# Window attention in a hybrid decoder layer: the softmax of both key heads of a unit as one chain over eight heads

## The chip, the cores and the metric

The kernel runs on one core of one Trainium2 chip. The core has a matrix engine (PE, whose weight loads are listed apart as PEld), a vector engine (DVE), a scalar engine (ACT), a general engine (POOL) and queues for transfers (DMA), most of them issued from SP. The metric is the device time of one execution in microseconds (us). One execution was also taken with the hardware profiler; every row below is from that one.

## The reference, cut to what matters

One inference step of one layer: a prompt of 2048 rows and a sample group of 8 x 8 rows. One projection of the normalized input gives q, k, v, a gate z and the inputs of a state-space branch. The change touches the window attention of the prompt: 16 query heads of 64 elements share 4 key heads (4 query heads to each), every query sees the 128 keys up to its own, and a learned sink for each head joins the softmax.

```python
def sink_attention(q, k, v, mask, sinks):
    s = jnp.einsum('bnqkgd,bnskd->bnkgqs', q, k).astype(jnp.float32) * (HEAD_DIM ** -0.5)
    s = jnp.where(mask[None, :, None, None], s, -jnp.inf)
    sk = sinks.astype(jnp.float32).reshape(N_KV_HEADS, KV_GROUP)[:, :, None, None]
    m = jnp.maximum(s.max(-1, keepdims=True), sk)
    p = jnp.exp(s - m)
    p = p / (p.sum(-1, keepdims=True) + jnp.exp(sk - m))
    return jnp.einsum('bnkgqs,bnskd->bnqkgd', p.astype(v.dtype), v)
...
o_a = window_attention_prompt(q, k, v, p['sinks'])   # prompt: blocks of 128 queries
p_a = (o_a * jax.nn.silu(z_a)) @ p['w_attn_proj'].astype(o_a.dtype)
```

## The kernel before, in words

The program has three stages. T1 (`phase_t1`) projects q, k, v and the gate z and does the window attention; S does the state-space branch; T2 does the output projections. In the profiled execution T1 lasts to 741 us, S to about 1950 us, T2 to the end.

T1 goes over four blocks of 512 rows, in each over two pairs of key heads, and in each over four units `tt` of 128 queries: 32 units. A unit is 128 queries against two key heads (`kvl` 0 and 1), each with four query heads. For each key head `attn_unit` does the following.

- Scores: eight matmuls of 256 columns (L541) into two PSUM tiles `sc` (the pool `sc1` has two). They hold the older and the newer 128 keys side by side; each query uses one of the two at each place, so ACT copies the newer half to the SBUF tile `s` (L547) and DVE writes the older half over it where it is seen (L548). `s` is 128 queries x 4 heads x 128 keys.
- Softmax: one DVE reduce for the maximum (L553), then the helper `softmax` (L378): the negative maximum `ng` (L380), the sink's part `es` (L382, L383), an exp for each head on ACT that also sums (L386), the denominator `den` on DVE (L387 to L389), and the scaling of each head, two heads on ACT (L391) and two on POOL (L393).
- Four transposes on PE (L558) into a PSUM tile `tr`, and one DVE product with the masks `halves` that writes both halves of `PT` (L560).

When both key heads are there, four matmuls of 512 columns (L570) form the unit's output `po`, DVE multiplies it with the gate (L581), and SP stores it.

Other places that the text speaks of: `za_tile` (gate columns of a pair; in block 2 it also does the columns of the sample group, which pass through the SBUF tile `zt`, one buffer, L447 to L451, and are stored to `zss_d`), `sample_cols` (likewise through `zt`, L425, stored to `qks_d`), `v_tile` (values, and 32 columns for the state-space branch through the tile `dtt`, one buffer of its own, L491), `q_tile` (transposes L515), the projections' matmuls (L186, L199, L210), and the split of raw weights into two parts, a cast on ACT (L150) and a subtraction on DVE (L151). At the start of S, L811 transposes `dA`, whose result is stored to `ac_d` and loaded again as `AB` and `EB`; L902 transposes `xT`.

The order in which instructions stand on each engine is not the order of the code: a scheduler lays the whole program out ahead of time from its own estimates of durations and from the pools' buffers, and each engine then runs its list strictly in that order. The units' softmax work is so laid among the matmuls of projections of the same and the next block.

Of the kernel before, what the change touches and what calls it, by code (L numbers as in the profile page):

```python
# [9 lines left out]
F32 = mybir.dt.float32  # L10
F32R = mybir.dt.float32r
AF = mybir.ActivationFunctionType
ALU = mybir.AluOpType
AX = mybir.AxisListType
# [3 lines left out]
P = 128  # L18
# [4 lines left out]
NT = TB // P  # L23
NH, NKV, HD, HG = 16, 4, 64, 4
# [54 lines left out]
def build(tc, nc, a, o, seq, phases=("T1", "S", "T2"), dbg=None):  # L79
# [296 lines left out]
        )  # L376

    def softmax(wk, s, mx, width, nsk, sk, n):  # L378
        ng = wk.tile([P, 4], F32, name="ng", tag="ng")
        V.scalar_tensor_tensor(out=ng[:, :n], in0=mx[:, :n], scalar=-1.0, in1=nsk, op0=ALU.mult, op1=ALU.min)  # L380
        es_ = wk.tile([P, 4], F32, name="es", tag="es")
        V.tensor_tensor(es_[:, :n], sk, ng[:, :n], ALU.add)  # L382
        A.activation(es_[:, :n], es_[:, :n], AF.Exp)  # L383
        den = wk.tile([P, 4], F32, name="den", tag="den")
        for i in range(n):
            A.activation(s[:, i, :width], s[:, i, :width], AF.Exp, bias=ng[:, i : i + 1], accum_out=den[:, i : i + 1])  # L386
        V.tensor_tensor(den[:, :n], den[:, :n], es_[:, :n], ALU.add)  # L387
        V.tensor_scalar(den[:, :n], den[:, :n], 2.0, None, ALU.mult)
        V.reciprocal(den[:, :n], den[:, :n])  # L389
        for i in range(min(n, 2)):  # L390
            A.activation(s[:, i, :width], s[:, i, :width], AF.Copy, scale=den[:, i : i + 1])  # L391
        for i in range(2, n):
            G.tensor_scalar(s[:, i, :width], s[:, i, :width], den[:, i : i + 1], None, ALU.mult)  # L393

    def phase_t1():
        with ExitStack() as es:
# [9 lines left out]
            qtp = pool("qtp", 3)  # L406
            kvp = pool("kvp", 1)
            zap = pool("zap", 2)
            sp = pool("sp", 5)
            ptp = pool("ptp", 2)  # L410
            smp = pool("smp", 2)
            mmp = pool("mm1", 3, space=PSUM)
# [66 lines left out]
            def v_tile(b, hT):  # L479
                if b == 0:  # L480
                    SY.dma_start(raw_dt, w_in[:, OFF_DT : OFF_DT + 32].rearrange("(k p) c -> p k c", p=P))
                raw, hl = wload([(0, w_in[:, OFF_V : OFF_V + 256])])
                split(hl[:, 0, :, 256:288], hl[:, 1, :, 256:288], raw_dt)
                if b > 0:
                    G.tensor_copy(vT[:, 0], vT[:, 4])
                dtt = wk.tile([P, NT, 32], F32, name="dtt", tag="dtt", bufs=1)
                for tt in range(NT):
                    ps = mmp.tile([P, 288], F32, name="mm", tag="mm")
                    proj_tm(ps, hl, 288, hT, tt)
                    A.copy(vT[:, tt + 1], ps[:, :256])  # L490
                    V.tensor_copy(dtt[:, tt], ps[:, 256:288])  # L491
                SY.dma_start(dt_d[b], dtt)
                if b == NB - 1:
                    SY.dma_start(o["v_win_p"], vT[:, 4])
                if b == sb:
                    sample_cols(raw, lambda t: [(vn_d[:, P * f : P * f + P], t[64 * f : 64 * f + 64]) for f in range(2)])
                    psd = mmp.tile([P, 32], F32, name="mm", tag="mm")
                    for k in range(KT):
                        for f in range(2):
                            PE.matmul(psd[64 * f : 64 * f + 64], hs[:, k], raw_dt[:, k], start=k == 0, stop=k == KT - 1)  # L500
                    V.tensor_copy(dts, psd)
# [25 lines left out]
            def attn_unit(b, pair, tt, qTs, zs):  # L527
                full = b * NT + tt > 0
                k0, W = (tt * P, 256) if full else ((tt + 1) * P, P)
                ws = (0, 1) if full else (1,)  # L530
                PTs = []
                po = trp.tile([P, HG, P], F32, name="tr", tag="tr")
                for kvl in range(2):
                    kv = 2 * pair + kvl
                    s = sp.tile([P, HG, P], F32, name="s", tag="s")
                    mx = smp.tile([P, HG], F32, name="mx", tag="mx")
                    for hh in range(2):
                        sc = scp.tile([P, 2, 256], F32, name="sc", tag="sc")
                        for h in range(2):
                            for i in range(2):  # L540
                                PE.matmul(  # L541
                                    sc[:, h, :W], qTs[kvl][:, 2 * hh + h], KTT[:, i, kv, k0 : k0 + W],
                                    start=i == 0, stop=i == 1,
                                )
                        if full:
                            sv = s[:, 2 * hh : 2 * hh + 2]
                            A.copy(sv, sc[:, :, P:])  # L547
                            V.copy_predicated(sv, older.unsqueeze(1).to_broadcast([P, 2, P]), sc[:, :, :P])  # L548
                        else:
                            for h in range(2):  # L550
                                masked_max(s, mx, 2 * hh + h, sc[:, h, :P], mask, P)
                    if full:
                        V.tensor_reduce(mx, s, AX.X, ALU.max)  # L553
                    softmax(smp, s, mx, P, nsink[:, 4 * kv : 4 * kv + 4], sink[:, 4 * kv : 4 * kv + 4], HG)
                    PT = ptp.tile([P, 2, HG, P], F32, name="PT", tag="PT")
                    tr = trp.tile([P, HG, P], F32, name="tr", tag="tr")
                    for hg in range(HG):
                        PE.transpose(tr[:, hg], s[:, hg], ident)  # L558
                    if full:
                        got = V.tensor_tensor(  # L560
                            PT, tr.unsqueeze(1).to_broadcast([P, 2, HG, P]),
# [803 lines left out]
```

## Time and profile before

| | us |
|---|---|
| median of 3 runs | 3145.01 (3144.47 to 3152.12) |
| the profiled execution's own time | 3143.59 |
| its span on the core | 3141.8 |
| PE busy in the span | 3059.9 (97%) |
| stage T1, PE busy in its first 742 us | 699.63 |

Times in the rows are from the start of the span. "Idle" of an engine is time in which no instruction of it ran; the releaser after `<-` is what ended it. In the orders and rows, L-numbers are lines of the kernel; in the changed kernel the lines of `attn_unit` stand 1 to 3 lines lower or higher (scores L540, transposes L561, `PT` L563, products L573, gate product L584; in S L814 for L811 and L905 for L902).

### The profile page before, as it was taken

Reading aid. Unit: us, or ns where it says so; the run is one execution under the profiler, and the core shown is the slowest. Engines: PE = TensorE matmul, PEld = TensorE weight load, DVE = VectorE, ACT = ScalarE, POOL = GpSimd, SP = SyncE. Lnnn points to the kernel's source line nnn. Section 1 sums busy time; section 2 is a strip of 40 time slices with the busy share of each in tenths; the row PEclk is TensorE's granted clock in tenths of the full one; section 3 lists DMA queues with packets and bytes.
Section 4 is the critical chain, followed back from the end, with each engine's and each line's share of the span. In section 5 each row is a group of like instructions: output and inputs, shape, how many; then the busy total and the mean of one; then the engine's idle time right before and its main releaser. Section 6 shows DMA issues by size and latency. Waiting matters only on the chain.

```text
span 3141.8 us, 49127 instructions
## 1 busy us (share of the span) xinstructions
PE 3059.9 (97%) x18982; PEld 2635.5 (84%) x18982; DVE 1918.5 (61%) x3142; ACT 1356.5 (43%) x2863; POOL 933.1 (30%) x925
## 2 busy tenths in 40 slices
PE   8999999998999999999999998999999999999999
PEld 7979797976999888778877877878878899999888
DVE  5868767677666666676666665456556644333433
ACT  4656545455555444444445453343333322222321
POOL 2425232432455444555554554100111110000000
PEclk9999999999999999999999998999999999999999
DMA  6635345254777755665666564455655663345443
GB/s 223 189 106 148 112 120 166 68 185 154 243 256 259 282 207 202 233 228 188 222 244 212 201 219 142 149 141 172 208 176 144 177 193 123 103 147 159 138 107 104
DMA packets 409986, 553.72 MB, mean 176 GB/s; under 512 B 34145, under 2 KB 347257, under 8 KB 399497
## 3 DMA queue, kind: packets, MB, share of 16 engines
q1 hardware_dynamic: 409752, 550.59, 54.1%
q8 instruction: 149, 2.44, 0.3%
q14 instruction: 85, 0.69, 0.1%
HBM read 445.31 MB, written 107.30 MB: 176 GB/s over the span
## 4 chain that ended last, share of the span: by engine, by line
PE 78%; DVE 8%; DMA 4%; POOL 4%; issue 3%; ACT 2%; SPq 0%; POOLq 0%; DVEq 0%; ACTq 0%
PE mm L199 49%; PE mm L210 13%; PE mm L186 6%; DVE acc L792 2%; PE tr L570 2%; PE sc L541 2%; DVE whl L151 1%; PE py L910 1%; POOL ws L913 1%; POOL L L889 1%; PE tr L558 1%; PE st L916 1%; PE po L898 1%; DMA v<-v_d 1%; DVE zs L929 1%
## 5 line engine op out<-in xcount | busy, mean ns | idle before, releaser
L199 PE MATMUL mm<-hT,whl 128*128 128x512 f32 (+1 forms) x6720 | 1341.4, 355 | 6.1 <-DVE whl L151 3.0
L199 PEld LDWEIGHTS mm<-hT,whl 128*128 128x128 f32 x6720 | 1117.5, 189 | 175.8 <-issue 7.4
L199 PE MATMUL mm<-ot,whl 128*128 128x512 f32 (+1 forms) x2880 | 567.9, 354 | 3.0 <-DVE whl L151 1.4
L199 PEld LDWEIGHTS mm<-ot,whl 128*128 128x128 f32 x2880 | 474.9, 188 | 74.0 <-DVE whl L151 2.9
L151 DVE TENSOR_TENSOR whl<-raw,whl 128x2048 fp32r<-128x2048 f32 (+1 forms) x172 | 366.7, 2137 | 266.5 <-ACT whl L150 259.4
L150 ACT CAST whl<-raw 128x2048 fp32r<-128x2048 f32 (+1 forms) x172 | 298.4, 1746 | 218.0 <-PE mm L199 101.2
L210 PE MATMUL mm<-whl,hT 128*128 128x256 f32 (+1 forms) x2304 | 303.5, 286 | 2.7 <-DVE dtt L491 2.2
L210 PEld LDWEIGHTS mm<-whl,hT 128*128 128x128 f32 x2304 | 286.8, 189 | 7.9 <-issue 4.1
L792 DVE SCALAR_TENSOR_TENSOR acc<-cr,cwb,acc 128x512 f32<-128x512 f32 x288 | 272.5, 948 | 27.3 <-ACT acc L787 24.9
L889 POOL TENSOR_TENSOR L<-L,cbm 128x1024 f32<-128x1024 f32 x64 | 162.2, 2546 | 146.5 <-DVE cbm L878 139.5
L210 PE MATMUL mm<-whl,ot 128*128 128x256 f32 (+1 forms) x1632 | 204.0, 284 | 0.0
L210 PEld LDWEIGHTS mm<-whl,ot 128*128 128x128 f32 (+1 forms) x1632 | 198.8, 188 | 3.7 <-issue 2.1
L186 PE MATMUL mm<-hT,whl 128*128 128x512 f32 x768 | 192.7, 400 | 2.2 <-ACT hT L295 2.1
L887 ACT ACTIVATE L<-AB,acs 128x128 f32<-128x128 f32 x512 | 157.5, 390 | 63.1 <-PE py L910 29.3
L186 PEld LDWEIGHTS mm<-hT,whl 128*128 128x128 f32 x768 | 141.2, 190 | 33.5 <-ACT hT L295 2.5
L859 DVE SCALAR_TENSOR_TENSOR zs<-th,mm 128x512 f32<-128x512 f32 (+1 forms) x80 | 45.6, 577 | 152.4 <-ACT th L858 151.9
L393 POOL TENSOR_SCALAR s<-s,den 128x128 f32<-128x128 f32 x128 | 79.3, 632 | 198.7 <-DVE den L389 144.1
L858 ACT ACTIVATE th<-mm 128x512 f32<-128x512 f32 (+1 forms) x80 | 40.0, 508 | 202.8 <-PE mm L199 196.7
L150 ACT CAST ot<-v 128x512 fp32r<-128x512 f32 x96 | 58.7, 620 | 159.5 <-DVE v L1231 81.0
L386 ACT ACTIVATE s<-s,ng 128x128 f32<-128x128 f32 x256 | 99.9, 394 | 39.9 <-DVE ng L380 32.6
L1231 DVE SCALAR_TENSOR_TENSOR v<-v,snw,rb 128x512 f32<-128x512 f32 x64 | 49.3, 786 | 97.6 <-DMA v<-v_d 97.4
L913 POOL TENSOR_TENSOR ws<-wx,ws 128x512 fp32r<-128x512 f32 x64 | 106.4, 1663 | 5.1 <-ACT ws L912 4.9
(324 smaller groups left out, 3899.6 us busy)
## 6 DMA issues: line engine op xcount, KB each, us to landing
raw<-in_w_in_dram SPq DMA_DIRECT2D x72, 1024.0 KB
whl<-w_dx SPq DMA_DIRECT2D x24, 2048.0 KB
whl<-w_dz SPq DMA_DIRECT2D x24, 2048.0 KB
hT<-h_d SPq DMA_DIRECT2D x80, 512.0 KB
AB<-ac_d SPq DMA_DIRECT2D x64, 512.0 KB
raw<-in_w_ssd_proj_dram SPq DMA_DIRECT2D x32, 1024.0 KB
whl<-w_dbc SPq DMA_DIRECT2D x12, 2048.0 KB
raw<-in_w_in_dram SPq DMA_DIRECT2D x40, 512.0 KB
```

Source lines behind the costliest of these rows:

```text
L150: A.copy(hi, src)
L151: V.tensor_tensor(lo, src, hi.bitcast(F32), ALU.subtract)
L186: PE.matmul(ps, hl[:, x, k, c0 : c0 + P], ht[:, y, :], start=first and i == 0, stop=last and i == n - 1,)
L199: PE.matmul(ps, hl[:, x, k, c0 : c0 + P], ht[:, y, lo : lo + n], start=i == 0, stop=i == 3 * len(hT) - 1,)
L210: PE.matmul(ps, ht[:, x, tt * P : tt * P + m], hl[:, y, k, :n], start=i == 0, stop=i == 3 * len(hT) - 1,)
L386: A.activation(s[:, i, :width], s[:, i, :width], AF.Exp, bias=ng[:, i : i + 1], accum_out=den[:, i : i + 1])
L393: G.tensor_scalar(s[:, i, :width], s[:, i, :width], den[:, i : i + 1], None, ALU.mult)
L541: PE.matmul(sc[:, h, :W], qTs[kvl][:, 2 * hh + h], KTT[:, i, kv, k0 : k0 + W], start=i == 0, stop=i == 1,)
L792: V.scalar_tensor_tensor(out=acc, in0=raw[:, k : k + TB], scalar=cwb[:, k, ct : ct + 1], in1=acc, op0=ALU.mult, op1=ALU.add)
L887: A.activation(L[:, h], AB[:, h], AF.Relu, scale=-1.0, bias=acs[:, hc.start + h : hc.start + h + 1])
L889: G.tensor_tensor(L, L, cbm[:, c].unsqueeze(1).to_broadcast([P, 8, P]), ALU.mult)
L913: G.tensor_tensor(ws[:, 1], wx, ws[:, 0].bitcast(F32), ALU.subtract)
```

## The change

The unit gets one tile `s` of eight heads for both key heads (the pool `sp` goes from five tiles of four heads to three of eight), and `mx`, `ng`, `es` and `den` are eight wide. All scores of the unit are evacuated first; then there is one reduce, one chain of small operations and one exp of the sinks for the unit, eight exps, and the scaling, the first four heads (key head 0) on ACT and the last four (key head 1) on POOL. Transposes and `PT` of both key heads come behind that. Apart from it, `dtt` takes its place in the one buffer of `zt`.

```diff
     def softmax(wk, s, mx, width, nsk, sk, n):
-        ng = wk.tile([P, 4], F32, name="ng", tag="ng")
+        ng = wk.tile([P, 8], F32, name="ng", tag="ng")
...
-        for i in range(min(n, 2)):
+        for i in range((n + 1) // 2):
             A.activation(s[:, i, :width], s[:, i, :width], AF.Copy, scale=den[:, i : i + 1])
-        for i in range(2, n):
+        for i in range((n + 1) // 2, n):
             G.tensor_scalar(s[:, i, :width], s[:, i, :width], den[:, i : i + 1], None, ALU.mult)
...
-            sp = pool("sp", 5)
+            sp = pool("sp", 3)
...
-                dtt = wk.tile([P, NT, 32], F32, name="dtt", tag="dtt", bufs=1)
+                dtt = wk.tile([P, NT, 32], F32, name="dtt", tag="zt", bufs=1)
...
+                s = sp.tile([P, 2 * HG, P], F32, name="s", tag="s")
+                mx = smp.tile([P, 2 * HG], F32, name="mx", tag="mx")
                 for kvl in range(2):
                     kv = 2 * pair + kvl
-                    s = sp.tile([P, HG, P], F32, name="s", tag="s")
-                    mx = smp.tile([P, HG], F32, name="mx", tag="mx")
                     for hh in range(2):
...
+                        at = HG * kvl + 2 * hh
                         if full:
-                            sv = s[:, 2 * hh : 2 * hh + 2]
+                            sv = s[:, at : at + 2]
...
-                    if full:
-                        V.tensor_reduce(mx, s, AX.X, ALU.max)
-                    softmax(smp, s, mx, P, nsink[:, 4 * kv : 4 * kv + 4], sink[:, 4 * kv : 4 * kv + 4], HG)
+                if full:
+                    V.tensor_reduce(mx, s, AX.X, ALU.max)
+                heads = slice(2 * HG * pair, 2 * HG * pair + 2 * HG)
+                softmax(smp, s, mx, P, nsink[:, heads], sink[:, heads], 2 * HG)
+                PTs = []
+                for kvl in range(2):
                     PT = ptp.tile([P, 2, HG, P], F32, name="PT", tag="PT")
...
-                        PE.transpose(tr[:, hg], s[:, hg], ident)
+                        PE.transpose(tr[:, hg], s[:, HG * kvl + hg], ident)
```

The instructions of PE, POOL and the transfers keep their numbers; DVE has 2952 in place of 3142 and ACT 2549 in place of 2581. The order of the rest of S and of T2 is the same on every engine; that of T1 and of the first 30 us of S is new. At three places it stands as follows.

PE at the end of block 1 (its last units, called 13, 14 and 15 below, before the keys and values of block 2). Before, from the product of unit 13 (the L210 are projections of block 2, the L449 transposes of `zt`):

```order
L570 MATMUL tr<-PT,vT 64x512 x4
L210 MATMUL mm<-whl,hT 128x288 x20
L558 MATMUL tr<-cst,s 128x128
L210 MATMUL mm<-whl,hT 128x288
L558 MATMUL tr<-cst,s 128x128 x2
L210 MATMUL mm<-whl,hT 128x288 x3
L558 MATMUL tr<-cst,s 128x128 x5
L210 MATMUL mm<-whl,hT 128x288 x24
L570 MATMUL tr<-PT,vT 64x512 x4
L449 MATMUL tr<-cst,zt 128x128
L210 MATMUL mm<-whl,hT 128x288 x24
L449 MATMUL tr<-cst,zt 128x128
```

After, from the last scores of the block:

```order
L540 MATMUL sc<-KTT,qT 128x256 x8
L573 MATMUL tr<-PT,vT 64x512 x4
L210 MATMUL mm<-whl,hT 128x288 x24
L561 MATMUL tr<-cst,s 128x128 x8
L573 MATMUL tr<-PT,vT 64x512 x4
L561 MATMUL tr<-cst,s 128x128 x8
L573 MATMUL tr<-PT,vT 64x512 x4
L449 MATMUL tr<-cst,zt 128x128 x2
L472 MATMUL tr<-cst,kd 128x128 x4
L210 MATMUL mm<-whl,hT 128x288 x27
```

Before, 72 matmuls of 288 columns stood between the product of unit 13 and the second L449; after, 24, and the two L449 stand together.

The end of the first pair of block 3 (units 26 and 27, before the query transposes L515 of the second pair). DVE before, and then after:

```order
L560 TENSOR_TENSOR PT<-tr,halves 128x1024
L151 TENSOR_TENSOR whl<-raw,whl 128x2048 x2
L151 TENSOR_TENSOR hT<-hs,hT 128x64 x4
L560 TENSOR_TENSOR PT<-tr,halves 128x1024
L151 TENSOR_TENSOR hT<-hs,hT 128x64 x2
L581 TENSOR_TENSOR zs<-tr,zs 128x4x128
```

```order
L563 TENSOR_TENSOR PT<-tr,halves 128x1024
L151 TENSOR_TENSOR whl<-raw,whl 128x2048 x2
L151 TENSOR_TENSOR hT<-hs,hT 128x64 x2
L548 COPY_PREDICATED s<-cst,sc 128x256
L151 TENSOR_TENSOR hT<-hs,hT 128x64
L548 COPY_PREDICATED s<-cst,sc 128x256
L151 TENSOR_TENSOR hT<-hs,hT 128x64 x3
L584 TENSOR_TENSOR zs<-tr,zs 128x4x128
L553 TENSOR_REDUCE mx<-s 128x8
L380 SCALAR_TENSOR_TENSOR ng<-mx,nsink 128x8
```

PE at the same place, before and then after (the L186 are the last matmuls of a projection):

```order
L541 MATMUL sc<-KTT,qT 128x256 x4
L186 MATMUL mm<-hT,whl 128x512 x17
L570 MATMUL tr<-PT,vT 64x512 x4
L558 MATMUL tr<-cst,s 128x128 x8
L570 MATMUL tr<-PT,vT 64x512 x4
L515 MATMUL tr<-cst,qr 128x128 x8
```

```order
L186 MATMUL mm<-hT,whl 128x512 x19
L561 MATMUL tr<-cst,s 128x128 x3
L540 MATMUL sc<-KTT,qT 128x256 x2
L561 MATMUL tr<-cst,s 128x128 x3
L540 MATMUL sc<-KTT,qT 128x256 x2
L561 MATMUL tr<-cst,s 128x128
L540 MATMUL sc<-KTT,qT 128x256 x2
L561 MATMUL tr<-cst,s 128x128
L540 MATMUL sc<-KTT,qT 128x256 x2
L573 MATMUL tr<-PT,vT 64x512 x4
L561 MATMUL tr<-cst,s 128x128 x8
L573 MATMUL tr<-PT,vT 64x512 x4
```

After, the second half of unit 27's scores and the transposes of unit 26 stand behind the last filler, and the evacuation of those scores stands on DVE behind two splits of weights for S.

PE at the start of S, before and then after (L199 are the projections of S):

```order
L570 MATMUL tr<-PT,vT 64x512 x4
L199 MATMUL mm<-hT,whl 128x288 x177
L811 MATMUL tr<-dA,cst 128x128
L812 MATMUL tr<-dA,ones 128x128
L813 MATMUL tr<-cst,dA 128x128
L199 MATMUL mm<-hT,whl 128x288 x63
```

```order
L573 MATMUL tr<-PT,vT 64x512 x4
L199 MATMUL mm<-hT,whl 128x288 x151
L814 MATMUL tr<-dA,cst 128x128
L815 MATMUL tr<-dA,ones 128x128
L816 MATMUL tr<-cst,dA 128x128
L199 MATMUL mm<-hT,whl 128x288 x41
```

The transposes of `dA` stand 26 matmuls earlier; from the first L199 to the transposes of `xT` there are 288 of these matmuls in both.

## Rows read from the trace of the kernel before

**Rows 1.** The profile's first part: busy time of each engine, share of the span, instructions.

```profile
PE 3059.9 (97%) x18982; PEld 2635.5 (84%) x18982; DVE 1918.5 (61%) x3142; ACT 1356.5 (43%) x2863; POOL 933.1 (30%) x925
```

**Rows 2.** Busy time by stretch: the stretch and its length, busy time (and instructions) of PE, PEld, DVE, ACT and POOL, the clock that PE was granted as a share of its full level, the busy share of the DMA engines, GB/s. The first row is all of T1, the second its last 42 us.

```profile
0.00:742.00 742.00, 699.63 (x4854) 596.72 (x4855) 529.91 (x1107) 399.70 (x1144) 247.54 (x312) 0.99 0.45 142
700.00:742.00 42.00, 31.08 (x175) 21.48 (x174) 28.95 (x79) 26.46 (x110) 9.89 (x19) 0.88 0.29 104
```

**Rows 3.** What PE waited for in T1: instruction and releaser, us in total, times, longest.

```profile
PE tr L570 <- DVE PT L560: 14.4, 8, 4.0
PE tr L558 <- ACT s L391: 5.0, 3, 2.6
PE tr L449 <- DVE zt L447: 0.3, 1, 0.3
```

**Rows 4.** DVE's work in T1 by line and shape: count, busy us, mean ns of one, and the idle time before them with its releaser.

```profile
L560 DVE TENSOR_TENSOR PT<-tr,halves 128x1024 f32<-128x1024 f32 x60 | 72.3, 1216 | 22.3 <-PE tr L558 22.1
L548 DVE COPY_PREDICATED s<-cst,sc 128x256 f32<-128x256 int32 x120 | 51.0, 442 | 5.5 <-ACT s L547 4.5
L553 DVE TENSOR_REDUCE mx<-s 128x4 f32<-128x512 f32 x60 | 40.8, 679 | 0.5
L387 DVE TENSOR_TENSOR den<-den,es 128x4 f32<-128x4 f32 x64 | 11.5, 182 | 34.7 <-ACT s L386 34.4
L382 DVE TENSOR_TENSOR es<-sink,ng 128x4 f32<-128x4 f32 x64 | 11.3, 177 | 1.2
L389 DVE RECIPROCAL den<-den 128x4 f32<-128x4 f32 x64 | 10.9, 170 | 0.7
L388 DVE TENSOR_SCALAR den<-den 128x4 f32<-128x4 f32 x64 | 10.4, 164 | 1.0
L380 DVE SCALAR_TENSOR_TENSOR ng<-mx,nsink 128x4 f32<-128x4 f32 x64 | 10.2, 159 | 0.8
```

**Rows 5.** The same of ACT and POOL.

```profile
L386 ACT ACTIVATE s<-s,ng 128x128 f32<-128x128 f32 x256 | 99.9, 394 | 39.9 <-DVE ng L380 32.6 <-DVE den L389 5.2 <-POOL s L393 1.3
L391 ACT ACTIVATE s<-s,den 128x128 f32<-128x128 f32 x128 | 44.4, 397 | 38.2 <-DVE den L389 34.3 <-DVE ng L380 3.3 <-DVE den L387 0.6
L383 ACT ACTIVATE es<-es 128x4 f32<-128x4 f32 x64 | 12.6, 196 | 0.6 <-DVE es L382 0.5
L393 POOL TENSOR_SCALAR s<-s,den 128x128 f32<-128x128 f32 x128 | 79.3, 632 | 198.7 <-DVE den L389 144.1 <-DVE ng L380 19.7 <-DVE es L382 10.9
```

**Rows 6.** PE in order of time at the end of block 1: start, us, line, what, count, and in brackets the idle time before with its releaser. (A product counts eight here, two passes of each of its four matmuls.)

```profile
390.59 1.94 PE L570 MATMUL tr<-PT,vT 128*64 128x512 f32 x8 [2.10 <-DVE PT L560]
393.39 2.93 PE L210 MATMUL mm<-whl,hT 128*128 128x288 f32 x20 [0.86 <-DVE dtt L491]
398.71 3.46 PE L210 MATMUL mm<-whl,hT 128*128 128x288 f32 x24 [0.98 <-DVE dtt L491]
```

**Rows 7.** DVE in order of time, just behind that: `zt` through its one buffer, and POOL's scaling of four heads.

```profile
404.69 0.28 DVE L451 SCALAR_TENSOR_TENSOR zt<-zt,tr 128x128 f32<-128x128 f32 x1
407.43 0.29 DVE L447 COPY zt<-mm 128x128 f32<-128x128 f32 x1 [2.46 <-DMA zss_d<-zt]
...
413.07 0.29 DVE L425 COPY zt<-mm 128x128 f32<-128x128 f32 x1 [1.67 <-DMA qks_d<-zt]
...
393.36 2.35 POOL L393 TENSOR_SCALAR s<-s,den 128x128 f32<-128x128 f32 x4 [7.47 <-DVE dtt L491]
```

**Rows 8.** PE, DVE and ACT in order of time at the end of the first pair of block 3.

```profile
674.15 4.11 PE L186 MATMUL mm<-hT,whl 128*128 128x512 f32 x17
...
683.26 0.84 PE L558 MATMUL tr<-cst,s 128*128 128x128 f32 x4 [2.56 <-ACT s L391]
688.12 3.68 PE L570 MATMUL tr<-PT,vT 128*64 128x512 f32 x8 [4.01 <-DVE PT L560]
691.73 1.45 PE L515 MATMUL tr<-cst,qr 128*128 128x128 f32 x8
...
681.91 4.48 DVE L151 TENSOR_TENSOR whl<-raw,whl 128x2048 fp32r<-128x2048 f32 x2
```

**Rows 9.** PE in order of time in the second pair of block 3, the last of T1, and the first projection of S.

```profile
711.03 1.19 PE L541 MATMUL sc<-KTT,qT 128*128 128x256 f32 x8 [0.76 <-DVE s L548]
...
732.02 3.68 PE L570 MATMUL tr<-PT,vT 128*64 128x512 f32 x8 [3.12 <-DVE PT L560]
735.64 1.67 PE L558 MATMUL tr<-cst,s 128*128 128x128 f32 x8
739.20 1.94 PE L570 MATMUL tr<-PT,vT 128*64 128x512 f32 x8 [1.89 <-DVE PT L560]
741.07 23.78 PE L199 MATMUL mm<-hT,whl 128*128 128x288 f32 x177
```

**Rows 10.** The start of S: PE in order of time, and of the chain of work that ended last the transfers of `dA`'s result.

```profile
764.68 0.38 PE L811 MATMUL tr<-dA,cst 128*128 128x128 f32 x2
786.93 0.48 PE L902 MATMUL tr<-cst,xT 128*128 128x128 f32 x1 [4.07 <-DVE xT L797]
...
766.47 7.59 DMA ac_d<-at
776.91 4.65 DMA EB<-ac_d
```

**Rows 11.** PE in order of time at the end of block 0.

```profile
225.66 0.84 PE L558 MATMUL tr<-cst,s 128*128 128x128 f32 x4 [2.06 <-ACT s L391]
```

More of the change, by code (lines that the diff above doesn't have):

```diff
@@ L378, in softmax @@
     def softmax(wk, s, mx, width, nsk, sk, n):
-        ng = wk.tile([P, 4], F32, name="ng", tag="ng")
+        ng = wk.tile([P, 8], F32, name="ng", tag="ng")
         V.scalar_tensor_tensor(out=ng[:, :n], in0=mx[:, :n], scalar=-1.0, in1=nsk, op0=ALU.mult, op1=ALU.min)
-        es_ = wk.tile([P, 4], F32, name="es", tag="es")
+        es_ = wk.tile([P, 8], F32, name="es", tag="es")
         V.tensor_tensor(es_[:, :n], sk, ng[:, :n], ALU.add)
         A.activation(es_[:, :n], es_[:, :n], AF.Exp)
-        den = wk.tile([P, 4], F32, name="den", tag="den")
+        den = wk.tile([P, 8], F32, name="den", tag="den")
         for i in range(n):
@@ L530, in attn_unit @@
                 ws = (0, 1) if full else (1,)
-                PTs = []
                 po = trp.tile([P, HG, P], F32, name="tr", tag="tr")
+                s = sp.tile([P, 2 * HG, P], F32, name="s", tag="s")
+                mx = smp.tile([P, 2 * HG], F32, name="mx", tag="mx")
                 for kvl in range(2):
                     kv = 2 * pair + kvl
-                    s = sp.tile([P, HG, P], F32, name="s", tag="s")
-                    mx = smp.tile([P, HG], F32, name="mx", tag="mx")
                     for hh in range(2):
@@ L550, in attn_unit @@
                             for h in range(2):
-                                masked_max(s, mx, 2 * hh + h, sc[:, h, :P], mask, P)
-                    if full:
-                        V.tensor_reduce(mx, s, AX.X, ALU.max)
-                    softmax(smp, s, mx, P, nsink[:, 4 * kv : 4 * kv + 4], sink[:, 4 * kv : 4 * kv + 4], HG)
+                                masked_max(s, mx, at + h, sc[:, h, :P], mask, P)
+                if full:
[4 more added lines that the diff above has]
+                for kvl in range(2):
                     PT = ptp.tile([P, 2, HG, P], F32, name="PT", tag="PT")
```

## The prediction, made before the changed kernel was run

> **What bounds the kernel now.** The busy shares come first: PE is busy 97% of the span, DVE 61%, ACT 43%, POOL 30% [rows 1]. So a microsecond saved on DVE or ACT is worth something only where PE waits for it. The change lies in T1, and the stretches say what there is to win: of its first 742 us PE works 699.63, so it is idle for 42.4, while DVE has 742 - 529.91 = 212 us of slack and ACT 342 [rows 2]. The list of waits then says what ends PE's idle time: 14.4 us in 8 waits for `PT`, 5.0 us in 3 waits for scaled scores [rows 3]. These two are ends of the softmax chain of a unit, and they come where a block's or pair's last units have too few projection matmuls left to stand between them. The last look is at those places in order of time: the end of block 0 [rows 11], the end of block 1 [rows 6], the end of block 3's first pair [rows 8] and its second pair, where in 42 us PE is busy 31.08 [rows 2, 9]. Everywhere else PE has filler while a softmax runs, and the length of the chain is of no account there.
>
> **What the change saves.** On DVE five kinds of small operations fall by 32 each, from 64: at 159 to 182 ns [rows 4] that is 32 x (182 + 177 + 170 + 164 + 159) = 27.3 us. Of the 60 reduces 30 remain, at double width. No row has that width for a reduce; its bounds are 0.68 us (width costs nothing) and 1.36 (twice); the nearest row by elements is the `PT` product, 1.22 us for 1024 [rows 4], and I take 1.2. That saves 40.8 - 36 = 4.8 us. ACT saves 32 x 196 ns = 6.3 us [rows 5]. Exps, scalings, evacuations and everything on PE keep their numbers. These 38 us all fall on engines with slack, so by themselves they are worth nothing; what counts is when the last result of a chain arrives.
>
> **What it lengthens.** Before, the chain of one key head from its last evacuation is: reduce 0.68, `ng` 0.16, four exps 4 x 0.39, `den` 0.5, two scalings on POOL 2 x 0.59 (four take 2.35 [rows 7]), in all 4.1 us, and the other key head's chain runs beside it on other engines. After, it is one chain: reduce 1.2, `ng` 0.16, eight exps 3.15, `den` 0.5, four scalings on POOL 2.35, in all 7.4 us, and nothing of key head 0 goes to PE before the exps of key head 1 are done [durations from rows 4, 5, 7]. Behind it two `PT` products now follow one another (2.4 us) where before the first was mostly done early. Where PE has 5 us of filler more than it needed, this costs nothing; where it has none, it costs up to 7.4 - 4.1 + 1.2 = 4.5 us a unit.
>
> One page speaks against the change: the Trainium skill, "Perfetto Trace Analysis", section "Optimizing Scalar/DVE Operations", says that grouping into larger operations can raise throughput when the engine is saturated, but that when it is not and causes bubbles on others, smaller instructions can let work finish sooner. With DVE busy 71% of T1, this trace is the second case [rows 2]. By the first half of the rule the sum would be the saving alone; that is the rival below.
>
> **The places, with the new order.** Each is followed through the order after with the durations of the rows.
>
> *End of block 1.* Behind the product of unit 13 only one group of 24 filler matmuls is left (3.46 us [rows 6]) and then transposes, product, transposes, product of units 14 and 15 with nothing between. A product can start 0.84 us (four transposes) plus two `PT`, 3.2 us, after the transposes begin; the eight transposes fill 1.5 to 1.7 of that [rows 9], so PE idles about 1.6, twice: 3.3. The transposes of unit 14 wait for the chain of 7.4; PE covers it with eight scores (1.2 [rows 9]), a product (1.94) and the filler: 6.6. If DVE did nothing else, the wait is 0.8; but between this unit's operations DVE has two `PT`, a split of 2.3 us and the reduce of unit 15, 5.9 us; if all of it delays, the wait is 6.7. Going through the order I get 4.2, and 0.5 at the transposes of unit 15. Together 8.0, against 2.10 + 0.86 + 0.98 = 3.9 before [rows 6]: +4.1. After waits of this kind PE ran a product in 3.68 us in place of 1.94 at its lower clock [rows 8, 9]; one such adds 1.7. I take **+5.5** (0 to +10).
>
> *The two L449.* The second needs `zt` again, which waits for the store of the first: ACT 0.28, L451 0.28, the transfer 2.46, L447 0.29 [rows 7], 3.3 us. Before, 24 matmuls (3.46 us) lay between and PE waited 0.3 [rows 3]; after, nothing does: **+3** (+2 to +3.3). `dtt` in `zt`'s buffer puts round trips of 1.7 to 2.5 us [rows 7] into DVE's list in block 2, before the copies that free PE's result tiles; three of these tiles hold PE for 3 x 3.46 us, so most is hidden: **+1** (0 to +5).
>
> *End of block 3's first pair.* Before, the filler ends at 674.15 + 4.11 = 678.26 and the query transposes start at 691.73 [rows 8]. After, eight scores and eight transposes of unit 26 and 27 have moved behind the filler, so it ends about 2.2 us sooner, at 676.1. From there, with t from the filler's end: transposes and scores, the first `PT` and its neighbours, to t = 4.6; the two splits 4.48 [rows 8], which have no cover now because the evacuation of unit 27 stands behind them: 9.1; evacuation, small splits and the gate product to 11; reduce 12.2, exps 15.7, `den` 16.3, POOL 18.6, last transposes 18.9, last `PT` 20.1, product to 22.0 or, at the lower clock, 23.8. So 698.1 to 699.9, that is **+7** (+3 if the copies are laid well, +9).
>
> *Second pair of block 3.* Four units without filler; before, it takes 741.07 - 691.73 = 49.3 us [rows 8, 9]. Going through the new order with the shortest durations gives 50.7, with the full ones 54.9; since DVE also has 4 us less to do here, **+1.5** (-3 to +5.6).
>
> *End of block 0 and products with little behind their transposes.* In block 0 PE waited 2.06 us for scaled scores [rows 11] and now waits for the longer chain: **+1** (0 to +3). In three more units the product stands 0.1 to 1.5 us of PE work behind the second head's transposes, where two `PT` need 2.4: **+2** (0 to +4).
>
> *Start of S.* The transposes of `dA` stand 26 matmuls of 23.78 / 177 = 0.134 us [rows 9] earlier behind the product: 3.5 us. The transfers behind them (7.59 and 4.65 us [rows 10]) end earlier by as much, and with them the one wait of 4.07 us for `xT` [rows 10]: **-3.5** (-4 to 0).
>
> Sum: 5.5 + 3 + 1 + 7 + 1.5 + 1 + 2 - 3.5 = +17.5. Against the profiled execution's own 3143.59 that is 3161; this execution lies 1.4 us under the median of the runs. What this measurement can tell from no change is about 0.3%, 9.4 us, the spread of the runs before being 7.6.
>
> **Rivals.**
>
> *Faster: the DVE is what paces the seams.* In the last 42 us of T1 DVE is busy 28.95 us [rows 2]; if at seams its list, not the chain, decides, each of some ten uncovered units gains its share of the saving, 32 / 32 = 1 us, and with the start of S the sum is -10 - 3.5: 3130. For it speaks that DVE's small operations wait in line behind `PT` and splits; against it that DVE idles 34.7 us before `den` for ACT's exps [rows 4], which stay as long as they were. It decides if the eight-head chain stays within what PE has left at all four seams. Chance 0.15.
>
> *No difference to speak of.* The scheduler's fillers cover the chain better than my walk says: the terms at block 1 and 3 shrink to their lower ends (0 and +3), and the start of S pays for the L449: 0 + 3 + 3 - 3.5 = +2.5, 3146. For it: PE's total idle in T1 is only 42 us and the matmuls are the same. Chance 0.17.
>
> *The filler is gone altogether.* All upper ends at once in blocks 1 and 3 (10 + 9 + 5.6 = 24.6), the others as taken (3 + 1 + 1 + 2 - 3.5 = 3.5), and 7 us of PE's work at half its clock, which adds 7: +35, 3179. For it: the clock is 0.88 over the last 42 us already [rows 2]. Chance 0.10.
>
> *Forecast*, +10 to +28: 0.58.
>
> **How the numbers follow.** Faster by over 0.3% is the first rival, 0.15; within 0.3% the second, 0.17; slower the other two, 0.68. The range goes from the value of no change, just under the own time, since less than 2 in 10 lies below, up to the last rival: 3142 to 3180. The forecast's own range is 3153 to 3171.
>
> **What would show it.** In the profile after: DVE with 2952 instructions and about 32 us less busy; PE's busy time unchanged; its waits for `PT` and for scaled scores in T1 up from 19.4 us together to above 30; a wait of about 3 us at the second L449; the query transposes of block 3's second pair 6 to 9 us later against the filler; T1 ending near 762; the wait for `xT` at the start of S nearly gone. I am wrong if these waits shrink, which would mean that the small operations on DVE, not the exps, set the seams; or if they grow but PE's idle time elsewhere falls by as much.

## The result, and the profile after

The changed kernel takes 3183.59 us (median of 4 runs, 3181.68 to 3186.37) against 3145.34 (4 runs, one more than in the table ahead): 1.0114 times the time before, 95% interval 1.0099 to 1.0129, or 38 us more. The direction was forecast; the size, +17.5 us with an upper end of 3180, was not.

The first part of the profile after, which answers to [rows 1], then its stretches, which answer to [rows 2] (T1 now lasts to 779 us):

```profile
PE 3071.9 (96%) x18982; PEld 2639.8 (83%) x18982; DVE 1903.0 (60%) x2952; ACT 1351.0 (42%) x2831; POOL 946.6 (30%) x925
```

```profile
0.00:780.00 780.00, 710.48 (x4853) 599.85 (x4854) 512.99 (x918) 394.05 (x1112) 257.43 (x312) 0.97 0.43 135
700.00:780.00 80.00, 50.80 (x265) 31.58 (x265) 47.81 (x93) 40.33 (x148) 14.76 (x25) 0.83 0.42 150
```

DVE has the 190 instructions less that the change says, and ACT 32 less: 2831 for 2863 (the 2549 and 2581 given with the change leave out 282 instructions that the profile counts, nearly all of them reads of an exp's sum). DVE is 15.5 us less busy, not the 32 that were named as a sign: the durations of its reduces and small operations fall by 30 together, but neighbours overlap at their ends, so the engine's busy time falls by less. In T1 PE is idle for 69.5 us in place of 42.4, which is 27 us. The other 11 us are in its busy time, 710.5 for 699.6 with the same instructions: the granted clock of the stretch fell from 0.99 to 0.97. The rest of the program is as long as before within 4 us (these two executions lie 41.8 us apart, the medians 38). What PE waited for in T1, as in [rows 3]:

```profile
PE tr L561 <- ACT s L391: 18.0, 3, 10.4
PE tr L573 <- DVE PT L563: 17.0, 12, 2.2
...
PE sc L540 <- DVE s L548: 6.7, 7, 2.0
...
PE tr L449 <- DVE zt L447: 3.4, 1, 3.4
```

Scaled scores are now the longest wait (18.0 us where it was 5.0), and scores wait longer for DVE's evacuation (6.7 us; before one wait of 0.8, and 2.8 us in two waits that the profile puts down to `den` on DVE). Of DVE's groups in [rows 4], the reduce of 1024 elements took 1.213 us, where the prediction had bounded it between 0.68 and 1.36 and taken 1.2.

```profile
L553 DVE TENSOR_REDUCE mx<-s 128x8 f32<-128x1024 f32 x30 | 36.4, 1213 | 0.4
```

Where the time went, by the start of the same transposes in the traces (us lost in each stretch against the kernel before; the last two columns are experiments e1 and e2 below, one half of the change each):

| stretch | forecast | change | `dtt` in `zt` alone | joined chain alone |
|---|---|---|---|---|
| to the first key transposes of block 1 | +1 | +9.1 | +0.7 | +7.7 |
| to the query transposes of block 1's second pair | 0 | 0.0 | 0.0 | 0.0 |
| to the first query transposes of block 2 | +9.5 | +14.2 | +8.7 | +4.4 |
| to the first key transposes of block 3 | +2 | -0.7 | +0.8 | -0.1 |
| to the query transposes of block 3's second pair | +7 | +10.1 | +1.7 | +9.9 |
| to the first projection after T1's last product | +1.5 | +5.3 | +1.1 | +5.1 |
| to the last wait for `xT` at the start of S | -3.5 | -0.1 | +0.1 | -0.2 |
| sum | +17.5 | +37.9 | +13.1 | +26.9 |

(The forecast does not place the three units of its +2; they are put into the fourth row.)

### The profile page after: what moved, and what is told of

Read it like the earlier page. It is cut to its first block, busy times and chain, and to the rows that moved or that the text cites. A ratio compares the mean times of both kernels' runs of the same rounds, so it can differ in the third digit from the quotient of the medians.

```text
span 3183.6 us, 48826 instructions
## 1 busy us (share of the span) xinstructions
PE 3071.9 (96%) x18982; PEld 2639.8 (83%) x18982; DVE 1903.0 (60%) x2952; ACT 1351.0 (42%) x2831; POOL 946.6 (30%) x925
## 4 chain that ended last, share of the span: by engine, by line
PE 76%; DVE 9%; DMA 5%; POOL 4%; ACT 3%; issue 3%; SPq 0%; POOLq 0%; DVEq 0%; ACTq 0%
PE mm L199 48%; PE mm L210 12%; PE mm L186 5%; DVE acc L795 2%; PE tr L573 2%; PE sc L540 1%; DMA hT<-h_d 1%; DMA raw<-in_w_in_dram 1%; DVE whl L151 1%; PE py L913 1%; POOL L L892 1%; POOL ws L916 1%; PE st L919 1%; ACT L L890 1%; PE po L901 1%
## 5 line engine op out<-in xcount | busy, mean ns | idle before, releaser
L199 PE MATMUL mm<-hT,whl 128*128 128x512 f32 (+1 forms) x6720 | 1342.1, 356 | 8.0 <-DMA hT<-h_d 4.0
L199 PEld LDWEIGHTS mm<-hT,whl 128*128 128x128 f32 x6720 | 1118.2, 189 | 178.3 <-issue 8.1
L199 PE MATMUL mm<-ot,whl 128*128 128x512 f32 (+1 forms) x2880 | 568.9, 355 | 3.7 <-ACT ot L150 2.4
L199 PEld LDWEIGHTS mm<-ot,whl 128*128 128x128 f32 x2880 | 476.1, 189 | 74.4 <-ACT ot L150 3.3
L210 PE MATMUL mm<-whl,hT 128*128 128x256 f32 (+1 forms) x2304 | 303.2, 287 | 1.7 <-issue 1.7
L210 PEld LDWEIGHTS mm<-whl,hT 128*128 128x128 f32 x2304 | 287.3, 190 | 4.9 <-issue 4.4
L892 POOL TENSOR_TENSOR L<-L,cbm 128x1024 f32<-128x1024 f32 x64 | 162.5, 2549 | 143.8 <-DVE cbm L881 137.9
L210 PE MATMUL mm<-whl,ot 128*128 128x256 f32 (+1 forms) x1632 | 204.0, 284 | 0.0
L210 PEld LDWEIGHTS mm<-whl,ot 128*128 128x128 f32 (+1 forms) x1632 | 198.8, 188 | 3.7 <-issue 2.1
L186 PE MATMUL mm<-hT,whl 128*128 128x512 f32 x768 | 193.6, 403 | 4.2 <-ACT hT L295 2.3
L186 PEld LDWEIGHTS mm<-hT,whl 128*128 128x128 f32 x768 | 142.2, 191 | 39.4 <-issue 3.4
L393 POOL TENSOR_SCALAR s<-s,den 128x128 f32<-128x128 f32 x128 | 87.0, 696 | 207.1 <-DVE den L389 158.0
L799 ACT ACTIVATE th<-acc 128x512 f32<-128x512 f32 x96 | 60.3, 628 | 110.5 <-DVE acc L795 110.4
```

What stands on the lines that cost most here:

```text
L186: PE.matmul(ps, hl[:, x, k, c0 : c0 + P], ht[:, y, :], start=first and i == 0, stop=last and i == n - 1,)
L199: PE.matmul(ps, hl[:, x, k, c0 : c0 + P], ht[:, y, lo : lo + n], start=i == 0, stop=i == 3 * len(hT) - 1,)
L210: PE.matmul(ps, ht[:, x, tt * P : tt * P + m], hl[:, y, k, :n], start=i == 0, stop=i == 3 * len(hT) - 1,)
L892: G.tensor_tensor(L, L, cbm[:, c].unsqueeze(1).to_broadcast([P, 8, P]), ALU.mult)
```

## The experiments

**Which half: `dtt` in the buffer of `zt`, and the joined chain.**

```diff
-                dtt = wk.tile([P, NT, 32], F32, name="dtt", tag="dtt", bufs=1)
+                dtt = wk.tile([P, NT, 32], F32, name="dtt", tag="zt", bufs=1)
```

e1 is the kernel before with this line alone; e2 is the change without it. To make room, e2 also writes the negative maximum over `mx` in place of a tile `ng`.

> The kernel before with one edit, dtt in the buffer of zt. Theory A (the shared buffer is a large part by itself: the copies of dtt must wait until zt is done with, so the matmuls of the values of block 2 cannot be laid between the last units of block 1, which lose their filler): 10 to 14 us over the kernel before, all of it between the last units of block 1 and the query transposes of block 2, 3155 to 3159. Theory B (the chain over eight heads is what costs, the shared buffer only adds round trips of zt): +3 to +5, 3148 to 3150.

> The changed kernel with dtt in a buffer of its own again (the negative maximum is written over mx to make room). Theory A: 10 to 14 us under the changed kernel, 3170 to 3174, with filler again between the last units of block 1. Theory B: 3 to 5 under it, 3179 to 3181.

e1 took 3156.39 us, 1.0033 (1.0020 to 1.0045) times before, +10. e2 took 3175.18, 1.0087 (1.0072 to 1.0102), 8 us under the change, which is between the ranges of the two theories; its profiled execution (3164.61) was the fastest of its six, so its column above adds up to less than its median. By e1, theory A holds: the shared buffer is not 3 to 4 us of round trips but about 10. Of the 13.1 in its profiled execution 8.7 lie at the end of block 1. PE in e1 there:

```profile
391.26 1.94 PE L570 MATMUL tr<-PT,vT 128*64 128x512 f32 x8 [2.10 <-DVE PT L560]
394.37 1.76 PE L558 MATMUL tr<-cst,s 128*128 128x128 f32 x7 [1.17 <-ACT s L391]
...
398.18 3.68 PE L570 MATMUL tr<-PT,vT 128*64 128x512 f32 x8 [1.32 <-DVE PT L560]
401.79 0.48 PE L449 MATMUL tr<-cst,zt 128*128 128x128 f32 x1
405.68 0.45 PE L449 MATMUL tr<-cst,zt 128*128 128x128 f32 x1 [3.41 <-DVE zt L447]
406.63 5.43 PE L210 MATMUL mm<-whl,hT 128*128 128x288 f32 x28
```

The 48 filler matmuls (projections that PE can do while a softmax runs) that stood between these two products, and the 24 between the two L449, now all stand behind the second L449. `dtt` is copied out of the projection of the values; in `zt`'s buffer it can start only when `zt` is through, so the scheduler could not lay those matmuls ahead. In e2, which has the joined chain, those 24 are back between the two L449, and PE waits 0.28 us at the second:

```profile
419.85 0.33 PE L449 MATMUL tr<-cst,zt 128*128 128x128 f32 x1 [0.28 <-DVE zt L447]
```

So the loss of filler that the prediction charged to the joined chain in block 1 came from this line.

**The tile, and which link of the chain.** e3 keeps the tile of eight heads and `dtt` in `zt` but has two chains; e4 joins only the front (evacuation, reduce, `ng`, `es`); e5 joins only the end (denominator, scaling); e9 has the reduce by key head and the rest joined; e8 splits the scaling anew.

```diff
# e3, in the loop over the key heads, behind their evacuation
+        V.tensor_reduce(mx[:, own], s[:, own], AX.X, ALU.max)
+        softmax(smp, s[:, own], mx[:, own], P, ..., HG)
+        turn(kvl)                      # transposes and PT of this key head
# e4, in softmax, behind one ng and es for eight heads
+        for j in range(0, n, 4):       # four exps, den, two scalings each on ACT and POOL
# e5, in the loop over the key heads; den and scaling behind it for eight
+        V.tensor_reduce(mx[:, own], s[:, own], AX.X, ALU.max)
+        softmax_exps(s, mx, own, ...)  # ng, es and four exps
+    softmax_den(s, 2 * HG, sms)
# e9, in the loop over the key heads; softmax stays joined
+        V.tensor_reduce(mx[:, own], s[:, own], AX.X, ALU.max)
# e8, in softmax
-        for i in range((n + 1) // 2):
+        for i in range(n): if i % 4 < 2: A.activation(...) else: G.tensor_scalar(...)
```

> The changed kernel with its tile of eight heads, its pools and dtt in the buffer of zt, but the softmax done for each key head by itself as before (reduce, small operations, four exps, two scalings on ACT and two on POOL, transposes). If the chain is what costs apart from dtt, this is equal to the kernel before with dtt in the buffer of zt, within 0.1%. If the wider tile with three buffers costs, it is slower than that by what it costs, up to the 38 us of the whole change.

> The changed kernel with the denominator and the scaling done for each key head behind its own four exps, two heads on ACT and two on POOL; evacuation, reduce, ng and es stay in one for both. Theory C (key head 0 waits for the exps of key head 1 and for four scalings in a row): the chain of key head 0 is 1.6 us of exps and 1.2 us of scalings shorter; over some ten units without filler 10 to 20 us under the changed kernel, 3164 to 3174. Theory D (what costs is that the evacuation and the reduce wait for the scores of both): within 5 us of the changed kernel, 3179 to 3184.

> The changed kernel, but each key head's reduce, ng, es and exps follow its own evacuation; only the denominator and the scaling (key head 0 on ACT, key head 1 on POOL) and what comes behind them stay in one for both. Theory D (what costs is that nothing of key head 0 starts before the scores of key head 1 are evacuated): nearly all of what the joined chain costs is gone; the two-chain kernel took 3153.6, and the joined scaling adds 3 to 8 us, so 3156 to 3162. If any waiting of key head 0 for key head 1 costs, also that for the denominator: 3168 or more.

> The changed kernel with one edit: the reduce is done for each key head behind its own evacuation, all the rest (ng, es, exps, denominator, scaling) stays joined. Theory D1 (what counts is that the exps of key head 0 wait for the maximum of key head 1): the last reduce is half as wide, 0.5 us less a unit, the rest stays: 3174 to 3184. Theory D2 (what counts is the reduce over eight heads that stands on DVE behind all four evacuations): most of the 22 us between this change and the kernel with exps by key head (3158.7) are gone: 3160 to 3166.

> The changed kernel with the scaling split within each key head, two heads on ACT and two on POOL, the rest as in the change. Key head 0's transposes can then start after two ACT scalings and two on POOL (1.2 us) in place of four on ACT (1.2 to 1.6), and key head 1's after two more of each, in place of four on POOL (2.35). At the six places where PE waited for scaled scores in the change this is worth at most 1.2 us each where POOL was last: 3178 to 3184.

| | us (median) | ratio to before |
|---|---|---|
| e3 two chains, tile of eight | 3153.60 | 1.0022 (1.0012 to 1.0032) |
| e5 end joined | 3158.70 | 1.0035 (1.0022 to 1.0049) |
| e4 front joined | 3180.31 | 1.0110 (1.0096 to 1.0124) |
| the change, all joined | 3183.59 | 1.0114 (1.0099 to 1.0129) |
| e8 all joined, scaling 2 + 2 | 3185.46 | 1.0120 (1.0106 to 1.0134) |
| e9 all joined, reduce by key head | 3187.30 | 1.0130 (1.0115 to 1.0146) |

e3 equals e1 within the spread, so the tile and its pool cost nothing that can be measured. e4 keeps nearly the whole loss, e5 nearly none of it: D holds. e4 by itself says nothing on C, since the scheduler laid all eight exps of a unit ahead of the first scaling there, in each of the 32 units. C falls by e5, where too all eight exps of a unit stand ahead of its scaling, and the cost is gone. e9 then tells its two forms apart: with the reduce by key head nothing is won (it came out 3 us above even D1's range), so it is not the wide reduce (D2) but that the first exp of key head 0 waits for the maximum of key head 1 (D1). e8 shows that the split of the scaling, in which the prediction had seen 1.2 us a unit, is worth nothing that can be measured. PE's waits in T1, first e5 (its products are L593, transposes L581), then e4 (L576, L564):

```profile
PE tr L593 <- DVE PT L583: 12.1, 7, 4.0
...
PE tr L581 <- ACT s L409: 6.2, 4, 3.2
```

```profile
PE tr L576 <- DVE PT L566: 16.3, 12, 2.2
PE tr L564 <- ACT s L394: 15.5, 5, 8.5
```

In e5 both are near where they were in [rows 3] (one more wait of a product, 3.8 us, is put down to a split of `hT`); in e4 the wait for scaled scores is 15.5 us. ACT in e4, the last of the eight exps at the end of block 3's first pair and the first scaling behind it:

```profile
717.80 0.39 ACT L389 ACTIVATE s<-s,ng 128x128 f32<-128x128 f32 x1
...
718.19 0.68 ACT L394 ACTIVATE s<-s,den 128x128 f32<-128x128 f32 x2
```

**Do the two causes add?** e11 is e5 with `dtt` in its own buffer and, as in e2, the negative maximum written over `mx`.

> The kernel with exps by key head and joined denominator (3158.7) with dtt in its own buffer. If the two causes add, the 8 to 10 us of the shared buffer fall away: 3148 to 3151, within 0.3% of the kernel before. If not, it stays above 3154.

It took 3147.63, 1.0002 (0.9992 to 1.0012): the joined denominator and scaling are free, and with the two causes out nothing of the 38 us is left.

**Is it only the last units?** e6 has two chains in 14 units next to places without filler and the joined chain in 18; e7 is the complement; e12 has the joined chain only in 12 units of blocks 1 and 2. 

```diff
# two chains, else the joined one, if
+ e6   (pair, tt) in ((0, 3), (1, 2), (1, 3)) or b == NB - 1 and pair == 1
+ e7   not ((pair, tt) in ((0, 3), (1, 2), (1, 3)) or b == NB - 1 and pair == 1)
+ e12  not (b == 2 or b == 1 and pair == 0)
```

> The changed kernel with two chains as before in 14 of its 32 units, those next to places where the filler runs out (the last of a block's first pair, the last two of its second pair, all of block 3's second pair), and the joined chain in the other 18. Theory: the joined chain costs only at those places, so all but a few us of the 30 between the two-chain kernel (3153.6) and the change (3183.6) are gone: 3154 to 3160. Rival (the joined chain costs wherever it is, because the scheduler lays everything anew): about 18 / 32 of it stays, 3170.

> The complement: the joined chain in those 14 units, two chains in the other 18. Theory: 3177 to 3184, as the change. Rival: about 14 / 32 of the 30 us, 3167.

> The changed kernel with the joined chain only in 12 units: the first pair of block 1 and both pairs of block 2, where in the trace of the change the query transposes of block 1's second pair and the keys of block 3 came no later against the key transposes and queries ahead of them than before; two chains in all other 20 units. Theory (the joined chain costs only in pairs whose filler runs out, but there in all of their units, since the units ahead delay the last ones): equal to the two-chain kernel (3153.6) within 4 us, 3150 to 3158. Rival (it costs wherever it is, by 12 / 32 of the 30 us): 3165.

e6 took 3172.91 (1.0078, 1.0065 to 1.0091), e7 3169.82 (1.0069, 1.0057 to 1.0082): 19 and 16 us over e3, where the theory had said nearly 0 and 30. It falls in that form. The rival, that the joined chain costs wherever it is, had said 16 and 13 and is within 3 us of both. The traces show where. In block 0, from the first key transposes to those of block 1, e3, e6 and e7 in turn:

```profile
60.42 0.60 PE L472 MATMUL tr<-cst,kd 128*128 128x128 f32 x4
237.74 0.66 PE L472 MATMUL tr<-cst,kd 128*128 128x128 f32 x4
```

```profile
60.13 0.60 PE L472 MATMUL tr<-cst,kd 128*128 128x128 f32 x4
247.56 0.66 PE L472 MATMUL tr<-cst,kd 128*128 128x128 f32 x4
```

```profile
58.95 0.60 PE L472 MATMUL tr<-cst,kd 128*128 128x128 f32 x4
237.63 0.66 PE L472 MATMUL tr<-cst,kd 128*128 128x128 f32 x4
```

These are 177.3, 187.4 and 178.7 us: the joined chain costs 10.1 us there in the five units ahead of the last ones (e6) and 1.4 in the other three (e7). In block 3's first pair either half costs nearly as much as both, 8.0 us in e6 and 8.5 in e7 against e3, where the whole change loses 9.6. Two rows of e6 at its end (the products are L585):

```profile
704.97 1.94 PE L585 MATMUL tr<-PT,vT 128*64 128x512 f32 x8 [2.34 <-DVE PT L543]
...
716.53 1.33 PE L541 MATMUL tr<-cst,s 128*128 128x128 f32 x4 [5.80 <-ACT s L391]
```

The last unit has two chains and its transposes still wait 5.80 us; the product of the unit ahead, which has the joined chain, waits 2.34, and the order at this place is that of the change: the last filler stands ahead of the second half of the last unit's scores. In e3 17 filler matmuls stand between those scores and that product, which does not wait. e12, 3161.11 (1.0043, 1.0029 to 1.0056), is 7.5 us over e3, between the 0 to 4 of the theory and the 11 of the rival; its trace is 4.0 us behind e3's at the start of S, of which 3.5 arise in block 1's first pair and nothing lasting in block 2. So the cost is lower where filler lasts, but not nothing. How it divides over units stays open: each of these kernels is laid anew by the scheduler, and the chain could not be lengthened with the order held.

**The other direction.** e10 is the kernel before with reduce, `ng` and exps for every two heads.

```diff
+        two = slice(2 * hh, 2 * hh + 2)      # in the loop over hh, behind the evacuation
+        V.tensor_reduce(mx[:, two], s[:, two], AX.X, ALU.max)
+        front(s, mx, two, ...)               # ng and two exps
```

> The other direction, from the kernel before: reduce, ng and exps follow each evacuation of two heads at once; es, denominator and scaling stay for four heads. DVE gets 64 small operations of 0.16 us and 60 more reduces more, about 18 us. Theory D1 carried further (an earlier first exp shortens what is exposed where filler ends): 3 to 10 us under the kernel before, 3136 to 3143. Rival (the last evacuation sets the chain, and with four heads the wait for it is already short): within 3 us of before, or slower by DVE's extra work at the seams, up to 3156.

3147.34, 0.9993 (0.9984 to 1.0002): no gain. Here an earlier first exp is worth something only up to the key head. No kernel here beats the one before.

## Why the prediction was wrong, point by point

**Right in kind.** The forecast's cause, a joined chain that PE has to wait for where filler ends, is there, and DVE's saving on slack was worth nothing. Of the signs named ahead, the waits for `PT` and scaled scores (35.0 us for 19.4) and the one at the second L449 (3.4) came; PE's busy time was to be unchanged and grew by 12 us, T1 was to end near 762 and ended at 779, and the wait for `xT` stayed (3.90 us for 4.07).

**What failed.** The step that failed first is the sentence that everywhere else PE has filler while a softmax runs, and the length of the chain is of no account there: by e6, 19 of the 30 us of the joined chain stay when the units next to those places have two chains, and block 0, of which only the end was walked, is the term most mis-sized. The second is `dtt` in `zt`'s buffer, taken at 1 us (with 3 more in the L449 term, not put down to it), which costs 10. The third is the start of S, which gives nothing back. Of the chain itself, 7.4 us for 4.1, not every part costs: the scaling of four heads on POOL (1.2 us; e8, e5 and e11) and the wider reduce (0.5 us; e9) make no difference, nor does it that nothing of key head 0 goes to PE before the exps of key head 1 are done, which holds in e11 too. What is left, by elimination, is that the four exps of key head 0 (1.6 us) stand behind the last evacuation.

**The Trainium skill's rule, and the rivals.** e5 has more instructions on DVE than the change and is 25 us faster; e10, which breaks up further, gains nothing. The rule of the Trainium skill (Perfetto Trace Analysis, section Optimizing Scalar/DVE Operations) is that breaking up instructions may let work finish sooner when these engines are not saturated but cause bubbles on others; e5 agrees with it, and e10 shows no more to win. The rivals "faster" and "no difference" fell; the last rival's +35 is nearest in size, though its causes (block 1 from the chain, the tail) are not how the loss divides.

**End of block 3's first pair: walked well, +7 forecast, +10.1 measured.** PE and DVE of the change at this place, answering [rows 8]:

```profile
696.08 4.58 PE L186 MATMUL mm<-hT,whl 128*128 128x512 f32 x19
...
717.00 2.52 PE L561 MATMUL tr<-cst,s 128*128 128x128 f32 x8 [10.45 <-ACT s L391]
720.86 3.68 PE L573 MATMUL tr<-PT,vT 128*64 128x512 f32 x8 [1.33 <-DVE PT L563]
724.47 1.09 PE L515 MATMUL tr<-cst,qr 128*128 128x128 f32 x8
...
704.48 4.48 DVE L151 TENSOR_TENSOR whl<-raw,whl 128x2048 fp32r<-128x2048 f32 x2
...
710.96 1.21 DVE L553 TENSOR_REDUCE mx<-s 128x8 f32<-128x1024 f32 x1
```

From the filler's end (700.66) to the query transposes it is 23.8 us, the end of the walk with the lower clock (23.8). The two splits and the reduce stand as told, and the last transposes end 18.9 us behind the filler, as walked; PE's wait for them is 10.45 us. What was wrong is the start: the filler was to end 2.2 us sooner, and against block 3's first key transposes it ends only 0.3 sooner (76.05 us behind them for 76.31).

**End of block 1 and the L449: +9.5 forecast, +14.2 measured, and put down to the wrong edit.** The rows of the change are the walked ones. The first wait is a little shorter than walked (3.71 us for 4.2), the two for `PT` (2.23 and 2.12 for 1.6 each) and the one at L449 a little longer, and two products run at the lower clock where one was in the sum:

```profile
394.55 3.47 PE L210 MATMUL mm<-whl,hT 128*128 128x288 f32 x24
401.73 1.97 PE L561 MATMUL tr<-cst,s 128*128 128x128 f32 x8 [3.71 <-ACT s L391]
405.93 3.68 PE L573 MATMUL tr<-PT,vT 128*64 128x512 f32 x8 [2.23 <-DVE PT L563]
409.54 1.48 PE L561 MATMUL tr<-cst,s 128*128 128x128 f32 x8
413.14 3.08 PE L573 MATMUL tr<-PT,vT 128*64 128x512 f32 x8 [2.12 <-DVE PT L563]
416.15 0.47 PE L449 MATMUL tr<-cst,zt 128*128 128x128 f32 x1
420.04 0.30 PE L449 MATMUL tr<-cst,zt 128*128 128x128 f32 x1 [3.41 <-DVE zt L447]
```

The L449 term (+3) was right in size but not put down to the `dtt` line, from which it comes: the wait is 3.41 us in e1 and 0.28 in e2. The step that failed is "`dtt` in `zt`'s buffer: +1": e1 prices the line at 8.7 us here, and the joined chain alone costs 4.4, for which 5.5 were taken.

**Block 0: +1 forecast, +9.1 measured: the term most mis-sized.** Only the end of the block was walked. First the change, then two rows of before:

```profile
174.22 2.28 DVE L151 TENSOR_TENSOR whl<-raw,whl 128x2048 fp32r<-128x2048 f32 x1
176.53 1.28 DVE L521 TENSOR_TENSOR qT<-tr,qT 64x512 fp32r<-64x512 f32 x2
...
177.27 0.66 PE L540 MATMUL sc<-KTT,qT 128*128 128x128 f32 x4 [2.68 <-DVE qT L521]
...
232.91 3.60 PE L573 MATMUL tr<-PT,vT 128*64 128x512 f32 x8 [2.12 <-DVE PT L563]
```

```profile
170.52 1.28 DVE L521 TENSOR_TENSOR qT<-tr,qT 64x512 fp32r<-64x512 f32 x2 [0.50 <-ACT qT L520]
...
174.36 2.28 DVE L151 TENSOR_TENSOR whl<-raw,whl 128x2048 fp32r<-128x2048 f32 x1
```

Of the 9.1 us 0.9 arise ahead of the first key transposes, before any unit. PE waits 1.47 us for a load of `hT` that it did not wait for before. The pair's last unit ends later, and on DVE a split of weights now stands ahead of the queries of the next pair, where it stood behind them: PE waits 2.68 us. Then two products wait, and the second runs 3.60 us at the lower clock. By e6 and e7 it is mostly the units ahead of the last ones that bring this about.

**Second pair of block 3: +1.5 forecast, +5.3 measured**, near the far end of its bounds (5.6): it takes 54.7 us, the walk with full durations (54.9), not the shortest ones (50.7), nearer to which the term was taken. **The clock**: one slow product (1.7 us) was in the sum; PE's busy time in T1 grew by 11 us.

**Start of S: -3.5 forecast, -0.1 measured.** PE, DVE, SP's queue and the store of `at` (`dA`'s result) in the change, then SP's queue before:

```profile
779.12 20.33 PE L199 MATMUL mm<-hT,whl 128*128 128x288 f32 x151
799.29 0.38 PE L814 MATMUL tr<-dA,cst 128*128 128x128 f32 x2
824.84 0.47 PE L905 MATMUL tr<-cst,xT 128*128 128x128 f32 x1 [3.90 <-DVE xT L800]
...
800.66 0.28 DVE L820 COPY at<-tr 128x128 f32<-128x128 f32 x1
...
799.64 0.32 SPq L173 DMA_DIRECT2D w_dz<-whl  x1
800.01 3.32 SPq L157 DMA_DIRECT2D raw<-in_w_in_dram  x2
803.42 3.46 SPq L821 DMA_DIRECT2D ac_d<-at  x1
...
811.98 0.80 SPq L887 DMA_DIRECT2D AB<-ac_d  x2
...
803.42 8.51 DMA ac_d<-at
```

```profile
761.58 0.32 SPq L173 DMA_DIRECT2D w_dz<-whl  x1
...
766.47 2.35 SPq L818 DMA_DIRECT2D ac_d<-at  x1
...
774.08 0.79 SPq L884 DMA_DIRECT2D AB<-ac_d  x2
```

The transposes of `dA` do stand 3.4 us earlier (20.2 us behind the first projection for 23.6), but the store of their result to `ac_d` stands in SP's queue behind a store of 2 MB of weights, which is tied to the split, and behind two loads of weights, whose issue takes 3.32 us. The 2 MB store is issued 20.5 us behind the first projection in both. So `at`, ready at 800.94, waits in the list until 803.42: its store is issued only 1.1 us sooner than before (24.3 us behind the first projection for 25.4), and takes 8.51 us to land, for 7.59 before [rows 10]. `AB` is loaded 32.9 us behind the first projection after, 33.0 before. The step did not count the queue that the store has to pass. The Trainium skill (DMA: Bandwidth & Descriptors, section Queues, rings and completion order) says that on each transfer engine descriptors are consumed in ring order. The trace agrees in so far as 64 KB, issued 1.1 us sooner behind the same 2 MB, landed only 0.2 us sooner.

## What to carry to other kernels

Joining two softmax chains saves instructions, but here it made the first exp of one half wait for the maximum of the other, and that cost 30 us; join what lies behind the exps (here free) and leave the front as it is. A tile moved into another's single buffer is an ordering edge: look at what else can then no longer be laid ahead, not only at the round trip that it adds. When units at the end of a stretch have no filler, the units ahead of the last ones count too; walk these as well.

## What the runs showed of the hardware

The price of the lower clock was larger than expected: with 27 us more idle time in T1, PE's busy time for the same instructions grew by 11 us and the granted clock of the stretch fell from 0.99 to 0.97; products behind waits took up to 3.68 us for 1.94. A reduce of 1024 elements to 8 results took 1.213 us, 1.8 times the 0.679 of 512 elements to 4. A small store gained 1.1 of the 3.4 us by which its result came sooner, and then took 0.9 us longer from issue to landing.
